# The early token tiles of the first head pair computed in float32r beside the conditioning

## The chip, the cores and the metric

The kernel runs on one core of a Trainium2 chip. TensorE (PE) multiplies matrices, VectorE (DVE), ScalarE (ACT) and GpSimd (POOL) do the elementwise work, and SyncE (SP) issues the loads and stores. The metric is the device time of one execution in microseconds (us). The kernel before takes 982.68 us, the median of three runs (982.2 to 984.94).

## The reference

One inference step of a diffusion layer: 128 prompt tokens and 1024 sample tokens, 1024 features, in float32. What matters for the front of the kernel:

```
a = silu(cond) @ w_ada + b_ada              # shift, scale, gate; one row per kind of token
h = rmsnorm(x) * norm_g * (1 + scale) + shift
q, k, v, ... = split(h @ w_in)              # 8 heads of 64 for q, k and v
q = rmsnorm(q per head) * q_norm_g ;  k = rmsnorm(k per head) * k_norm_g
```

q, k and v then go into windowed attention (sample tokens) or full attention (prompt tokens). Fourier mixing, pooling, gates and the output projection follow; the change does not touch them.

## The kernel before

The 1152 tokens are nine tiles of 128 (tiles 0 to 7 are sample tokens, tile 8 is the prompt). The front part runs once, before attention:

- *Loads* (one SP queue, in the written order): the small vectors, sixteen pieces of w_ada (`wa`, 512 KB each, for shift and scale), nine x tiles (`xt`, 512 KB), the four raw weight pieces of pair 0 (`wr_q`, 384 KB), and the first context keys and values (`kall`, `vall`).
- *Conditioning:* `ada_piece` multiplies silu(c) by a piece of w_ada in float32 (L398). After four pieces `ada_row` (ScalarE, L404) copies the row out as `ar`, `ada_end` turns it with four small matmuls `pb` (L410), and VectorE makes `sh` and `gs` (L416 to L419), shift and gain of two of the eight feature blocks k.
- *x:* `xnorms` squares a tile on ScalarE (L366) and takes the root on GpSimd (L367, L368); `xscale` scales it on VectorE (L372); `x_group` transposes three tiles at a time on TensorE (L385) into `xT`, by copies on VectorE and ScalarE (L386).
- *h:* `h_full` applies `gs` and `sh` (L451, L453). `scale_h` (L424 to L439, with the small matmuls `pbd` and `pbs`) finds from all of `gs` and `sh` one power of two, `shs`. `make_h` splits h times shs into two float16 parts: `hh` on ScalarE (L457), `hl` on VectorE (L458).
- *Weights:* `prep` squares the pieces (L86), gets a scale, and splits them into float16 parts (L112, L113).
- *Projection:* each product is three matmuls, high by high, high by low and low by high (L164 to L166). Pair 0 (two heads; q, k and v columns together 384) takes its first five token tiles at once, block k by block k, in five PSUM banks. `p1_done` then squares q and k (`sq`, L280), splits v (L281, L292), takes roots (`ss` L288, GpSimd L289 to L291), normalizes (`tk`, L295) and splits into float16 (`tok`, L302 on ScalarE, L305 on VectorE).

Tiles 8, 5, 6 and 7 of pair 0 follow one at a time. The tokens of the first four tiles are turned by transposes `pq` (L643) and `pk` (L658) as soon as their `tok` is ready, and attention starts.

The kernel is written under a manual schedule from before the loads on: every engine runs its instructions in the order of the program text. Each engine works off its queue in order, and the engines wait for each other by semaphores. `head_scales` (L479 to L494) and `v_scales` (L463 to L474) find the scales of cached keys and values with small matmuls between (`pkm`, `pks`, `pvm`, `pvs`); `new_pair` (L242 to L253) makes the constants of a pair.

Of the kernel before, what the change touches and what calls it, by code (L numbers as in the profile page):

```python
# [20 lines left out]
P = 128  # L21
# [14 lines left out]
NWA = 6  # L36
# [3 lines left out]
def mixer_layer(ctx: ExitStack, tc: tile.TileContext, xs, xp, smalls, qgrow, kgrow, bgate, wss, wgate, w1, w3, pw, wo,  # L40
# [74 lines left out]
    def prep(pieces, name):  # L115
# [3 lines left out]
        for i, src in enumerate(pieces):  # L119
            n = src.shape[-1]  # L120
            raw = wp.tile([P, WU], F32, tag="wr", name=f"wr_{name}{i}", bufs=NR)
            nc.sync.dma_start(raw[:, :n], src)
            raws.append(raw[:, :n])
        yield unit
# [56 lines left out]
    G.memset(mhalf, -0.5)  # L181

# [12 lines left out]
    with tc.tile_pool(name="hp", bufs=1, side="right") as hp:  # L195
        hh, hl = [], []
        for i in range(2):
            hh.append(hp.tile([P, 4, NT], F16, name=f"hh{i}"))
            hl.append(hp.tile([P, 4, NT], F16, name=f"hl{i}"))
# [28 lines left out]
        with tc.tile_pool(name="qkv", bufs=1) as qkv:  # L228
# [40 lines left out]
            def p1_done(c, t, pt, wait):  # L269
# [57 lines left out]
            man = ExitStack()  # L327
            man.enter_context(tc.manual_schedule())


            with tc.tile_pool(name="st", bufs=1) as st:
# [12 lines left out]
                def load_x(t):  # L344
                    xt[t] = st.tile([P, D], F32, tag="xt", name=f"xt{t}", bufs=6)
# [30 lines left out]
                XG = ((0, 1, 2), (3, 4, 5), (6, 7, 8))  # L376
                xT = st.tile([P, KT, NT], F32, name="xT")

                def x_group(ts):

                    n = len(ts) * P
                    for k in range(KT):
                        pt = bank(("s", "pt", "s")[k % 3], f"xt{k}_{ts[0]}")
                        for i, t in enumerate(ts):
                            T.transpose(pt[:, i * P:(i + 1) * P], xt[t][:, k * P:(k + 1) * P], ident)  # L385
                        (V.tensor_copy if k % 2 == 0 else S.copy)(xT[:, k, ts[0] * P:ts[0] * P + n], pt[:, :n])  # L386
# [3 lines left out]
                def ada_piece(i):  # L390
                    b, j = divmod(i, 4)
                    if j == 0:
                        pas[b] = bank("p1", f"pa{b}")
# [27 lines left out]
                def scale_h():  # L421
# [5 lines left out]
                    V.scalar_tensor_tensor(ab[:, 3:4], ab[:, 1:2], 31.0, ab[:, 2:3], op0=ALU.mult, op1=ALU.add)  # L427
                    pb = bank("po", "pbd")
# [4 lines left out]
                    V.tensor_scalar(md, ident[:2, :2], m1, None, op0=ALU.mult)  # L433
                    pb2 = bank("po", "pbs")
# [6 lines left out]
                    return hm  # L441

# [1340 lines left out]
```

## Time and profile before

| | |
|---|---|
| median of three runs | 982.68 us |
| profiled execution | 982.22 us |
| its span | 980.4 us |
| mean granted TensorE clock | 0.987 |
| TensorE busy | 918.3 us (94%) |
| VectorE busy | 656.3 us (67%) |
| ScalarE busy | 488.8 us (50%) |
| GpSimd busy | 202.4 us (21%) |

The profile is of one execution. Busy time is a share of the whole span; a stage of 100 us at the front can look quite different. Granted clock 1.00 stands for 2.4 GHz on TensorE, 0.50 for 1.2 GHz. A row of a timeline gives start, duration, engine, line, operation, output and inputs, and in brackets the idle time of the engine before it and what ended it. The duration of a matmul covers its way through a pipeline; the distance of two starts tells how fast they follow each other.

### The profile page before, as it was taken

How to read it: one execution, taken by the hardware profiler on the slowest of the kernel's cores; microseconds unless marked ns; L12 is line 12 of the kernel's file. 1: busy time of each engine (PE TensorE's matmuls, PEld its weight loads, DVE VectorE, ACT ScalarE, POOL GpSimd, SP SyncE). 2: the span in 40 equal slices, each digit the busy share in tenths (PEclk: the TensorE clock that was granted, in tenths of full speed). 3: DMA queues.
4: the chain of work that ended last, by engine and by line, in shares of the span. 5: the costliest groups of instructions: out<-in, count | busy, mean ns of one | idle time of the engine just before them, and what ended most of it. 6: DMA issues, size and time to landing. Idle time of an engine off the chain costs nothing.

```text
span 980.4 us, 17726 instructions
## 1 busy us (share of the span) xinstructions
PE 918.3 (94%) x6554; PEld 677.2 (69%) x6554; DVE 656.3 (67%) x1453; ACT 488.8 (50%) x1019; POOL 202.4 (21%) x340
## 2 busy tenths in 40 slices
PE   4778899999999999998997999999999999999998
PEld 2334467666666666665776779888888888877886
DVE  2348767777777546559778767478978789775322
ACT  2354757756856655665545545454555454442100
POOL 0000665245255322003102200002021020200000
PEclk9988999999999999999999999999999999999999
DMA  7730352151151151260249974543543432227321
GB/s 303 277 109 10 97 154 54 48 183 34 44 145 33 41 159 54 91 204 1 58 134 295 308 259 174 188 134 104 155 127 119 126 106 81 74 94 276 114 76 54
DMA packets 75783, 125.02 MB, mean 128 GB/s; under 512 B 12032, under 2 KB 45228, under 8 KB 75696
## 3 DMA queue, kind: packets, MB, share of 16 engines
q1 hardware_dynamic: 75695, 123.89, 39.2%
q8 instruction: 51, 0.84, 0.4%
q14 instruction: 37, 0.30, 0.1%
HBM read 88.20 MB, written 29.11 MB: 120 GB/s over the span
## 4 chain that ended last, share of the span: by engine, by line
PE 74%; DMA 8%; DVE 7%; ACT 5%; issue 3%; POOL 1%; SPq 1%; ACTq 0%; DVEq 0%; POOLq 0%
PE p L166 3%; PE p L164 3%; PE p L165 3%; PE wo L164 3%; PE wo L166 3%; PE wo L165 3%; PE m L164 3%; PE m L166 3%; PE m L165 3%; PE xc L164 3%; PE xb L164 3%; PE xb L166 3%; PE xb L165 3%; PE xc L165 3%; PE xc L166 3%; PE xa L164 3%
## 5 line engine op out<-in xcount | busy, mean ns | idle before, releaser
L164 PE MATMUL p<-wh_q,hh 128*128 128x384 f16 x288 | 95.1, 330 | 1.9 <-ACT hh L457 1.9
L166 PE MATMUL p<-wh_q,hl 128*128 128x384 f16 x288 | 95.0, 330 | 1.1 <-DVE hl L458 1.1
L165 PE MATMUL p<-wl_q,hh 128*128 128x384 f16 x288 | 95.1, 330 | 0.0
L733 DVE CUSTOM_DVE_ANT_0 sn<-s,bias 128x512 f32<-128x512 f32 x64 | 44.0, 688 | 31.4 <-PE s L729 30.5
L164 PE MATMUL m<-hh,wh_m 128*128 128x384 f16 x192 | 62.6, 326 | 0.0
L166 PE MATMUL m<-hh,wl_m 128*128 128x384 f16 x192 | 62.6, 326 | 0.0
L165 PE MATMUL m<-hl,wh_m 128*128 128x384 f16 x192 | 62.6, 326 | 0.0
L164 PE MATMUL wo<-woh,mh 128*128 128x512 f32 x144 | 56.8, 394 | 1.7 <-ACT woh L1536 1.7
L165 PE MATMUL wo<-wol,mh 128*128 128x512 f32 x144 | 56.6, 393 | 0.0
L166 PE MATMUL wo<-woh,ml 128*128 128x512 f32 x144 | 56.4, 392 | 0.0
L754 ACT CAST pts<-pt 128x512 f16<-128x512 f32 (+1 forms) x72 | 39.7, 552 | 29.2 <-PE pt L752 27.8
L758 DVE TENSOR_TENSOR pts<-pt,pts 128x512 f16<-128x512 f32 (+1 forms) x72 | 46.3, 642 | 3.7 <-ACT pts L754 3.1
L744 ACT ACTIVATE sn<-sn,mn 128x512 f32<-128x512 f32 x64 | 46.2, 722 | 3.9 <-DVE mn L733 3.9
L95 POOL TENSOR_SCALAR wsc_g<-wsc_g 128x1 f32<-128x1 f32 x12 | 2.6, 218 | 219.1 <-DVE wsc_g L94 219.1
L1665 DVE TENSOR_TENSOR yo<-wo,gb 128x512 f32<-128x512 f32 x18 | 12.4, 691 | 50.1 <-PE wo L166 50.0
L777 DVE TENSOR_SCALAR yt<-po,ri,vf 128x64 f32<-128x64 f32 x72 | 24.8, 344 | 29.7 <-PE po L773 26.4
L166 PEld LDWEIGHTS <-hl 128*128 128x128 f16 x288 | 28.4, 99 | 20.9 <-DVE hl L458 1.8
L164 PEld LDWEIGHTS <-hh 128*128 128x128 f16 x288 | 28.8, 100 | 19.0 <-ACT hh L457 2.0
L166 PEld LDWEIGHTS <-wl_m 128*128 128x128 f16 x288 | 28.3, 98 | 18.6 <-issue 0.4
L164 PEld LDWEIGHTS <-wh_m 128*128 128x128 f16 x288 | 28.9, 100 | 17.2 <-issue 0.6
L290 POOL TENSOR_TENSOR rs<-rs,mhalf 128x4 f32<-128x4 f32 x36 | 39.9, 1108 | 3.0
L165 PEld LDWEIGHTS <-hh 128*128 128x128 f16 x288 | 28.5, 99 | 17.1 <-issue 0.8
(650 smaller groups left out, 2942.5 us busy)
## 6 DMA issues: line engine op xcount, KB each, us to landing
wa<-in_wss_dram SPq DMA_DIRECT2D x16, 512.0 KB, 6.5
wr_q<-in_w_dram SPq DMA_DIRECT2D x16, 384.0 KB, 4.4
wr_m<-in_w_dram SPq DMA_DIRECT2D x24, 256.0 KB, 3.0
pp_c<-pec SPq DMA_DIRECT2D x24, 192.0 KB, 5.1
pp_b<-peb SPq DMA_DIRECT2D x24, 192.0 KB, 3.9
pp_a<-pea SPq DMA_DIRECT2D x24, 192.0 KB, 1.8
ppxc<-pp_c SPq DMA_DIRECT2D x16, 288.0 KB, 3.4
ppxb<-pp_b SPq DMA_DIRECT2D x16, 288.0 KB, 2.6
```

Source lines behind the costliest of these rows:

```text
L95: G.tensor_scalar(sc_[:, 2:3], sc_[:, 2:3], 1e-36, None, op0=ALU.max)
L164: T.matmul(out, lh, rh, start=first, stop=False)
L165: T.matmul(out, lh, rl, start=False, stop=False)
L166: T.matmul(out, ll, rh, start=False, stop=last)
L290: G.tensor_tensor(rs, rs, mhalf, op=ALU.pow)
L733: V.tensor_tensor_reduce(out=sn, in0=pS, in1=bt.rearrange("p a b -> p (a b)"), op0=ALU.add, op1=ALU.min, scale=1.0, scalar=3e38, accum_out=mn)
L744: S.activation(e[:, :n], it["sn"], AF.Exp, bias=it["mn"], scale=-1.0, accum_out=sm_)
L754: S.copy(pts[:, 0, :n], pt[:, :n])
L758: V.tensor_tensor(pts[:, 1, :n], it["pt"][:, :n], pts[:, 0, :n], op=ALU.subtract)
L777: V.tensor_scalar(yt[:, hd * 64:hd * 64 + 64], po[:, :64], ri, c["un"], op0=ALU.mult, op1=ALU.mult)
L1665: V.tensor_tensor(yo, pt, gb[0 if t == 8 else 1][:, cols], op=ALU.mult)
```

## The change

The first five token tiles of pair 0 (`NE` = 640 columns) no longer wait for all of the conditioning. For each block k, as soon as its `sh` and `gs` are there, `h_early` modulates 640 columns on VectorE (L468) and splits them into a float32r pair `eh` (ScalarE, L473) and `el` (VectorE, L476); `w_split` does the same with the raw weights (L491, L492). A float32r pair needs no scale. `p1_r` multiplies them in the same three matmuls, 128x384 (L168 to L170), and the steps k=0 to 7 stand between the pieces of the conditioning and the transposes.

x is transposed in groups of two, three, two and two tiles (a pair of tiles with two blocks k to a bank). There are four buffers for pieces of w_ada instead of six and five for x instead of six; `kall` and `vall` go into x buffers, and the loads are reordered. h in float16 is made after the early tiles, in the memory that `eh` and `el` leave: `make_h` on 512 columns (tiles 5 to 8), then on the early 640 (L483, L484), which pairs 1 to 3 read. The early tiles' roots are taken from unscaled products, with one more GpSimd multiply each (`gi`, L295). The manual schedule starts only behind all this; before it a scheduler orders the instructions.

```
-NWA = 6
+NWA = 4
+NE = 5 * P
...
+                    if "gi" in c:
+                        G.tensor_scalar(rs, rs, c["gi"], None, op0=ALU.mult)
...
-            man = ExitStack()
-            man.enter_context(tc.manual_schedule())
...
+                def x_group(ts, tags):
+                    n = len(ts)
+                    kk = 2 if n == 2 else 1
+                    for k in range(0, KT, kk):
+                        pt = bank(tags[nx[0] % len(tags)], f"xt{k}_{ts[0]}")
+                        for j in range(kk):
+                            for i, t in enumerate(ts):
+                                o = (j * n + i) * P
+                                T.transpose(pt[:, o:o + P], xt[t][:, (k + j) * P:(k + j + 1) * P], ident)
+                        (V.tensor_copy if nx[0] % 2 == 0 else S.copy)(xT[:, k:k + kk, ts[0] * P:(ts[0] + n) * P],
+                                                                       pt[:, :kk * n * P].rearrange("p (a b) -> p a b", a=kk))
+                        nx[0] += 1
...
+                def h_early(ks):
+                    for k in ks:
+                        h_part(k, slice(0, NE), 1)
+                        S.copy(ek(k)[0], xT[:, k, :NE])
+                    for k in ks:
+                        hi, lo = ek(k)
+                        V.tensor_tensor(lo, xT[:, k, :NE], hi.bitcast(F32), op=ALU.subtract)
+                def make_h(k, a):
+                    S.activation(hk(hh, k, a), xT[:, k, a], AF.Copy, scale=shs)
+                    V.scalar_tensor_tensor(hk(hl, k, a), xT[:, k, a], shs, hk(hh, k, a), op0=ALU.mult, op1=ALU.subtract)
...
+                def w_split(i, raw):
+                    hi = st.tile([P, WU], F32R, tag="wrh", name=f"wrh{i}", bufs=2)
+                    lo = st.tile([P, WU], F32R, tag="wrl", name=f"wrl{i}", bufs=2)
+                    S.copy(hi, raw)
+                    V.tensor_tensor(lo, raw, hi.bitcast(F32), op=ALU.subtract)
+                    wr_[i] = hi, lo
+                def p1_r(pt, t, k, first, last):
+                    eh, el = ek(k)
+                    a = slice(t * P, (t + 1) * P)
+                    b = slice((k % 2) * CH, (k % 2) * CH + CH)
+                    hi, lo = wr_[k // 2]
+                    mm3(pt[:, :CH], eh[:, a], el[:, a], hi[:, b], lo[:, b], first, last)
...
+                free = ("pt", "s", "p1")
+                ada(0, 1)
+                norm((0, 1))
+                ada(2, 3)
...
+                x_group((0, 1), free)
...
+                norm((2, 3, 4))
+                ada(4, 5, 6)
+                x_group((2, 3, 4), free)
+                w_split(0, raws[0])
+                h_early((0, 1))
+                ada(7)
...
+                pts = [bank(ebank[t], f"p1_0_{t}") for t in range(early)]
+                step(0)
...
+                w_split(1, raws[1])
+                h_early((2, 3))
+                norm((5, 6))
+                run(prep0, 4)
+                ada(8)
+                step(1)
+                ada(9)
+                step(2)
+                ada(10, 11)
...
+                x_group((5, 6), ("po",))
+                step(3)
...
+                w_split(2, raws[2])
+                h_early((4, 5))
...
+                norm((7, 8))
+                ada(12, 13)
+                step(4)
+                ada(14, 15)
...
+                wu0 = wu = run(prep0, 4)
+                x_group((7, 8), ("po",))
+                head_scales(kall)
+                v_scales(vall)
+                step(5)
...
+                w_split(3, raws[3])
+                h_early((6, 7))
...
+                    h_late(k, (S, V)[k % 2])
+                sc = scale_h()
+                next(sc)
...
+                        p1_r(pts[t], t, k, False, k == KT - 1)
+                    if t == 1:
+                        next(sc)
+                    if t == 3:
+                        next(sc, None)
+                ectx.close()
+                hp = hctx.enter_context(tc.tile_pool(name="hp", bufs=1, side="right", reuse_waits="tile"))
+                for i in range(2):
+                    hh.append(hp.tile([P, 4, NT], F16, name=f"hh{i}"))
+                    hl.append(hp.tile([P, 4, NT], F16, name=f"hl{i}"))
+                h_late(6, S)
+                h_late(7, V)
+                inverse_of(wu["sc"])
+                c0 = new_pair(0, wu)
+                gi = pers.tile([P, 1], F32, name="gi")
+                V.reciprocal(gi, wu["inv"])
+                c0e = dict(c0, gi=gi, i8=eighth, sv=c0["scv"])
+                for k in range(KT):
+                    make_h(k, slice(NE, NT))
+                for t in range(early):
+                    tick()
+                    tick()
+                    p1_done(c0e, t, pts[t], 8)
+                for k in range(KT):
+                    make_h(k, slice(0, NE))
+            man = ExitStack()
+            man.enter_context(tc.manual_schedule())
```

What the scheduler makes of it on TensorE, in the stretch of pieces 9 to 15 of the conditioning. In `pa2`, `pa3` the pieces' rows grow, `pb` turns them, `p1_0_0` is the bank of pair 0's tile 0. Before:

```order
L398 MATMUL pa2_337<-wa9_158,sil_83 32x512 x2
L398 MATMUL pa2_337<-wa10_160,sil_83 32x512 x2
L398 MATMUL pa2_337<-wa11_162,sil_83 32x512 x2
L410 MATMUL pb2_399<-pick_84,ar2_397 128x2 x4
L398 MATMUL pa3_421<-wa12_172,sil_83 32x512 x2
L130 MATMUL pw_q0_424<-wss_q0_408,onesp_75 128x4
L398 MATMUL pa3_421<-wa13_174,sil_83 32x512 x2
L398 MATMUL pa3_421<-wa14_176,sil_83 32x512 x2
L398 MATMUL pa3_421<-wa15_178,sil_83 32x512 x2
L410 MATMUL pb3_447<-pick_84,ar3_445 128x2 x4
```

After (numbers of buffers left out; `p_0_4` is tile 4's bank, `xt_5` a transposed bank of tiles 5 and 6):

```order
L168 MATMUL p_0_4_314<-wrh_339,eh_344 128x384
L405 MATMUL pa_371<-wa_158,sil 32x512 x2
L169 MATMUL p_0_4_314<-wrl_340,eh_344 128x384
L170 MATMUL p_0_4_314<-wrh_339,el_345 128x384
L390 MATMUL xt_5_412<-ident,xt_152 128x128
L390 MATMUL xt_5_412<-ident,xt_154 128x128
L390 MATMUL xt_5_412<-ident,xt_152 128x128
L390 MATMUL xt_5_412<-ident,xt_154 128x128
L168 MATMUL p_0_0_310<-wrh_339,eh_348 128x384
L169 MATMUL p_0_0_310<-wrl_340,eh_348 128x384
L170 MATMUL p_0_0_310<-wrh_339,el_349 128x384
```

Pieces that followed each other now stand alone between float32r matmuls of steps 2 and 3 and the transposes of tiles 5 and 6; before, no projection stood ahead of the last piece.

On VectorE, from the last `hl` to the first roots of pair 0's tiles, before (`gs4`, `grow` and `vf` are the pair's constants, `ss` the sums for the roots):

```order
L458 SCALAR_TENSOR_TENSOR hl1_98<-xT_121,shs_77,hh1_97 128x1152 x3
L242 TENSOR_SCALAR gs40_631<-qs__89,wsc_q0_428 128x2
L243 TENSOR_TENSOR grow0_630<-qgb_87,gs40_631 128x128
L242 TENSOR_SCALAR gs40_631<-ks__90,wsc_q0_428 128x2
L243 TENSOR_TENSOR grow0_630<-kgb_88,gs40_631 128x128
L247 TENSOR_SCALAR vf0_636<-wsc_q0_428 128x1
L248 TENSOR_TENSOR vf0_636<-vrec_79,wsc_q0_428 128x1
L249 TENSOR_TENSOR vf0_636<-vf0_636,svb_78 128x1
L90 TENSOR_SCALAR vf0_636<-vf0_636 128x1
L251 RECIPROCAL vf0_636<-vf0_636 128x1
L252 TENSOR_TENSOR vf0_636<-vf0_636,wsc_q0_428 128x1
L253 RECIPROCAL vf0_636<-vf0_636 128x1
```

After, where the 640-wide `hl` stand:

```order
L484 SCALAR_TENSOR_TENSOR hl1_692<-xT_114,shs_77,hh1_691 128x512
L256 RECIPROCAL vf0_705<-vf0_705 128x1
L484 SCALAR_TENSOR_TENSOR hl1_692<-xT_114,shs_77,hh1_691 128x512 x3
L297 SCALAR_TENSOR_TENSOR v160_713<-p1_0_0_310,vf0_705,v160_713 128x2x64
L297 SCALAR_TENSOR_TENSOR v160_713<-p1_0_1_311,vf0_705,v160_713 128x2x64
L297 SCALAR_TENSOR_TENSOR v160_713<-p1_0_2_312,vf0_705,v160_713 128x2x64
L297 SCALAR_TENSOR_TENSOR v160_713<-p1_0_3_313,vf0_705,v160_713 128x2x64
L300 TENSOR_TENSOR tk0_0_736<-p1_0_0_310,rg0_0_735 128x256
L484 SCALAR_TENSOR_TENSOR hl0_690<-xT_114,shs_77,hh0_689 128x640 x4
L484 SCALAR_TENSOR_TENSOR hl1_692<-xT_114,shs_77,hh1_691 128x640 x4
L291 TENSOR_REDUCE ss0_4_790<-sq0_4_789 128x4
```

All eight 640-wide `hl` now stand between the first `tk` and the first `tok` of the early tiles, and the 512-wide ones ahead of the early tiles' v; before, the last `hl` stood ahead of the pair's constants.

## Rows read from the trace of the kernel before

**Rows 1.** The page: engines' busy time, and a row of its DMA issues.

```profile
PE 918.3 (94%) x6554; PEld 677.2 (69%) x6554; DVE 656.3 (67%) x1453; ACT 488.8 (50%) x1019; POOL 202.4 (21%) x340
...
mk<-in_masks_dram SPq DMA_DIRECT2D x1, 576.0 KB, 3.3
```

**Rows 2.** Busy time by stretches: start:end, length, engines, granted clock, DMA share, GB/s.

```profile
48.00:64.00 16.00, 12.41 (x48) 6.01 (x48) 7.70 (x18) 8.89 (x17) 0.00 (x0) 0.92 0.36 99
75.00:78.00 3.00, 1.87 (x6) 0.68 (x7) 2.96 (x5) 3.00 (x3) 0.00 (x0) 0.50 0.00 0
96.15:115.25 19.10, 17.05 (x107) 10.09 (x105) 13.63 (x49) 12.05 (x31) 13.38 (x22) 1.00 0.50 133
```

**Rows 3.** Waits from 96 to 123: us in total, times, the longest.

```profile
PE pq L643 <- DVE tok L305: 1.6, 1, 1.6
...
PE pk L658 <- ACT q L645: 1.1, 1, 1.1
```

**Rows 4.** Timeline, VectorE and pq from 92 to 116: start, us, engine, line.

```profile
92.17 4.07 DVE L458 SCALAR_TENSOR_TENSOR hl<-xT,shs,hh 128x1152 f16<-128x1152 f32 x3
...
98.11 0.16 DVE L253 RECIPROCAL vf<-vf 128x1 f32<-128x1 f32 x1
...
104.34 0.42 DVE L305 TENSOR_TENSOR tok<-tk,tok 128x256 f16<-128x256 f32 x1 [0.47 <-ACT tok L302]
106.42 0.42 DVE L288 TENSOR_REDUCE ss<-sq 128x4 f32<-128x256 f32 x1 [1.66 <-ACT sq L280]
...
114.82 0.40 DVE L305 TENSOR_TENSOR tok<-tk,tok 128x256 f16<-128x256 f32 x1
115.28 0.45 PE L643 MATMUL pq<-id,tok 128*128 128x128 f16 x5 [1.64 <-DVE tok L305]
```

**Rows 5.** Timeline, ScalarE from 73 to 109.

```profile
73.71 3.55 ACT L457 ACTIVATE hh<-xT,shs 128x1152 f16<-128x1152 f32 x3 [3.01 <-DVE shs L90]
...
101.95 0.48 ACT L280 ACTIVATE sq<-p,vf 128x256 f32<-128x256 f32 x1 [0.24 <-PE p L166]
...
108.53 0.38 ACT L611 ACTIVATE kh<-kr,ks__90 128x128 f16<-128x128 f32 x1
```

**Rows 6.** Timeline of the conditioning and x, from 10 to 69.

```profile
10.72 1.06 ACT L366 ACTIVATE xsq<-xt 128x1024 bf16<-128x1024 f32 x1 [7.42 <-DMA xt<-in_xs_dram]
...
14.58 3.20 PE L398 MATMUL pa<-wa,sil 128*32 128x512 f32 x8 [3.20 <-DMA wa<-in_wss_dram]
...
15.83 2.08 DVE L372 TENSOR_SCALAR xt<-xt,xss 128x1024 f32<-128x1024 f32 x3 [11.76 <-POOL xss L368]
...
44.24 1.92 PE L398 MATMUL pa<-wa,sil 128*32 128x512 f32 x4
...
54.87 1.54 PE L385 MATMUL xt<-ident,xt 128*128 128x128 f32 x6 [0.57 <-ACT xT L386]
...
56.34 2.71 PE L398 MATMUL pa<-wa,sil 128*32 128x512 f32 x12
...
60.49 1.05 PE L410 MATMUL pb<-pick,ar 128*128 128x2 f32 x8 [1.43 <-ACT ar L404]
...
64.81 3.60 PE L398 MATMUL pa<-wa,sil 128*32 128x512 f32 x12
```

**Rows 7.** Timeline, TensorE at 147: float32 transposes of 128x128 (attention).

```profile
147.67 0.60 PE L752 MATMUL pt<-ident,sn 128*128 128x128 f32 x4
148.11 0.25 PE L773 MATMUL po<-v,pts 128*128 128x64 f16 x3
```

**Rows 8.** Timeline, TensorE at 447: float32r matmuls of 128x384 (the pooling branch).

```profile
446.99 0.34 PE L165 MATMUL yc<-dl,wph 128*128 128x384 f32 x1
447.16 0.34 PE L166 MATMUL yc<-dh,wpl 128*128 128x384 f32 x1
```

**Rows 9.** Timeline, VectorE: start and end of the head and value scales.

```profile
82.35 1.19 DVE L479 TENSOR_REDUCE km<-kall 64x8 f32<-64x1024 f32 x1
...
92.09 0.16 DVE L474 COPY vrec<-pvs 128x4 f32<-128x4 f32 x1 [0.47 <-PE pvs L473]
```

More of the change, by code (lines that the diff above doesn't have):

```diff
@@ L113, in split16, with prep @@
         V.scalar_tensor_tensor(lo, raw, sc_[:, 0:1], hi, op0=ALU.mult, op1=ALU.subtract)
-    def prep(pieces, name):
+    def prep(pieces, name, halves=False):
         unit = {"w": []}
@@ L123, in prep @@
             raws.append(raw[:, :n])
+            if halves and i == 1:
+                yield unit
+        unit["raws"] = raws
         yield unit
@@ L181, in mixer_layer @@
     G.memset(mhalf, -0.5)
+    eighth = pers.tile([P, 1], F32, name="eighth")
+    G.memset(eighth, 0.125)
     col = pers.tile([P, 44], F32, name="col")
@@ L193, in mixer_layer @@
     kb_ = pers.tile([P, 8], F32, name="kb_")
-    with tc.tile_pool(name="hp", bufs=1, side="right") as hp:
+    with ExitStack() as hctx:
         hh, hl = [], []
-        for i in range(2):
-            hh.append(hp.tile([P, 4, NT], F16, name=f"hh{i}"))
-            hl.append(hp.tile([P, 4, NT], F16, name=f"hl{i}"))
         def hk(z, k, a):
@@ L375, in mixer_layer @@
                 ebank = ["p1", "p1", "p1", "s", "pt"]
-                XG = ((0, 1, 2), (3, 4, 5), (6, 7, 8))
                 xT = st.tile([P, KT, NT], F32, name="xT")
[L379 to L386, printed above, removed]
+                nx = [0]
+                def x_group(ts, tags):
[10 more added lines that the diff above has]
+                        nx[0] += 1
                 pas = {}
@@ L455, in make_h, with ek @@
-                def make_h(k):
-                    a = slice(0, NT)
-                    S.activation(hk(hh, k, a), xT[:, k], AF.Copy, scale=shs)
-                    V.scalar_tensor_tensor(hk(hl, k, a), xT[:, k], shs, hk(hh, k, a), op0=ALU.mult, op1=ALU.subtract)
+                ectx = ExitStack()
+                ep = ectx.enter_context(tc.tile_pool(name="ep", bufs=1, side="right", reuse_waits="tile"))
+                ets = {}
+                def ek(k):
+                    if k not in ets:
+                        ets[k] = [ep.tile([P, NE], F32R, tag=x, name=f"{x}{k}", bufs=6) for x in ("eh", "el")]
+                    return ets[k]
@@ L494, in head_scales @@
                     V.tensor_copy(kb_, pks[:, :8])
-                prep0 = prep_pair(0)
-                wu0 = None
-                for what in ("w0", "w1", 0, 1, 2, "w2", "w3", 3, 4, 5, "w4", "w5", "w6", "w7", 6, 7, 8, "w8", "w9", "w10", "w11"):
-                    load_x(what) if isinstance(what, int) else load_wa(int(what[1:]))
-                run(prep0, 1)
-                for i in range(12, 16):
-                    load_wa(i)
-                kall = st.tile([64, 4, 2, P], F32, tag="wa", name="kall", bufs=NWA)
+                prep0 = prep([w1[0, i] for i in range(4)], "q0", True)
@@ new lines, in mixer_layer @@
+                for what in ("w0", "w1", 0, 1, "w2", "w3", 2, 3, 4, "r", "w4", "w5", "w6", "w7", "r", 5, 6, "w8", "w9", "w10", "w11",
+                             7, 8, "w12", "w13", "w14", "w15"):
+                    if isinstance(what, int):
+                        load_x(what)
+                    elif what == "r":
+                        r0 = run(prep0, 1)
+                    else:
+                        load_wa(int(what[1:]))
+                raws = r0["raws"]
+                kall = st.tile([P, D], F32, tag="xt", name="kall", bufs=5)[:64].rearrange("p (a h t) -> p a h t", a=4, h=2)
@@ new lines, in mixer_layer @@
+                h_late(6, S)
[7 more added lines that the diff above has]
+                    make_h(k, slice(NE, NT))
+                for t in range(early):
+                    tick()
+                    tick()
+                    p1_done(c0e, t, pts[t], 8)
```

91 lines of the change are left out of this document (22 added, 69 removed).

## The prediction, made before the result was known

> **What bounds the kernel now.** I read the page first: TensorE is busy for 918.3 of the 980.4 us of the span [rows 1], and after the first eighth that hardly varies. Whatever a change at the front wins must be found at the front. The busy time by stretches came next [rows 2]: TensorE works 12.41 of the 16 us from 48 to 64, at a rate looked at below. In the stretch 96.15 to 115.25 it has 17.05 of 19.1, VectorE 13.63 of the same 19.1. Third, TensorE's waits from 96 to 123 [rows 3]: the longest is 1.6 us, the transposes pq of pair 0's tokens waiting for VectorE's tok; the next is 1.1. Fourth, the timeline there [rows 4]: the fourth tok (tile 3) is issued at 114.82 and done at 115.22, and pq goes on at 115.28. From pq on both kernels run the same instructions in the same order (hl and hh are complete by then in both), so the change in time is, to first order, the change in when that tok ends. The reader should see that VectorE's queue, not the last matmul of the early tiles at about 101.9 [rows 5], opens that gate.
>
> **The change part by part.** All prices come from the profiled execution, 982.22 us (span 980.4); the median shown is 982.68, so 0.46 is added at the end.
>
> 1. *Until the transposes of tiles 2 to 4.* Two x tiles are loaded ahead of pieces 2 and 3 instead of three. Those pieces, waiting for their load, ended at 17.8 (14.58 + 3.20 [rows 6]); one tile less, about 1.3 of loading, gives 16.4. 16 transposes at 0.26 (six in 1.54 [rows 6]) end at 20.7. ScalarE squares tiles 2 to 4 from 19.8; three squares and GpSimd's two steps took from 10.72 to 15.83 [rows 6], and one copy (0.6) now stands between: 25.5. The first scaling (0.7, a third of 2.08 [rows 6]) gives 26.2.
>
> 2. *The interleaved stretch, steps k=0 to 5.* TensorE gets 56 transposes, 90 float32r matmuls, ten lone pieces and a pair, and two pb groups. At the upper clock: transposes 0.11 each (147.67 to 148.11 for four [rows 7]), 6.2; float32r passes of 128x384 0.17 to 0.175 (446.99 to 447.16 [rows 8]), 15.8; pb 2 x 1.05 = 2.1. A lone piece took 1.92 [rows 6] at the slow rate, three together 3.60; I halve the first as an estimate for ten lone ones and a pair, 11 x 0.96 = 10.6. Sum 34.7. What the clock does is the choice here. The profile prints 1.00 until 58, yet the same transposes go at 0.26 there and at 0.11 later [rows 6, 7], and 12 ada matmuls take 2.71 at 56.34 and 3.60 at 64.81 [rows 6]. So I read the first 56 us as the lower level (1.2 GHz), and the engine rose near 57 after a stretch of dense transposes from 48 on (12.41 busy of 16). The new stretch is at least as dense from 26.2. It could rise at once or after 10 us; I take 4.5, which do 2.25 us of work. 26.2 + 4.5 + 32.4 + 2.4 for two waits (ar, pb and VectorE's sh/gs behind a piece; 1.43 is one wait for ar [rows 6]) = 65.5. Were everything slow, it would be 26.2 + 69 + 2.4 = 98.
>
> The Trainium skill ("TensorE: Matmul & The Clock Gate", Part 4: PE-mode transpose) says that transposes do not engage the faster clock, as they do not count as busy "the same way". Here the rise near 57 came right behind transposes (the last six at 54.87 [rows 6]), so the trace speaks against it; by the page the interleaved stretch would stay slow longer, as in rival C.
>
> 3. *The scale chain.* After the last transposes VectorE runs copies, the head and value scales (82.35 to 92.25 in before, with TensorE round trips [rows 9]) and the modulation of the late columns between; a pb group stands behind the value scale in TensorE's order. I take 9.5, and k=6 begins at 75.
>
> 4. *k=6 and 7.* 30 float32r matmuls, begun after waits and so at the lower level: about 20 at 0.35 (twice 0.175, as 0.50 was granted from 75 to 78 behind a wait [rows 2]) and ten at 0.175, with pbd and pbs 0.84: 9.4. The early tiles end at 84.4, 17 us before they did; shs is there at 84.1.
>
> 5. *What is late next: VectorE.* The f16 pairs hh, hl were made under the early matmuls (hl 8 x 1.36, three in 4.07 [rows 4]); that cover is gone, because they now need shs, which comes when the early matmuls are over. They stand in the order between the early tiles' roots and toks, as the order excerpts show. A hl of 512 costs 0.69 and one of 640 0.83 (1.36 for 1152 [rows 4], less a fixed 0.16 or so, by width). From 84.1: twelve small instructions at 0.2 (eleven lie between the hl's end at 96.24 and 98.27 [rows 4]) to 86.5; eight hl of 512 and five small ones, 6.5, to 93.0; four v (0.30) and a tk, 1.6, to 94.6; eight hl of 640, 6.6, to 101.2. Then ss and v of tile 4, tok 0, tk and tok 1 with ScalarE's cast between: 103.0, against 104.76 before [rows 4]. From there to tok 3 the instructions are the same; they took 10.46, in which VectorE waits 1.66 for tile 8's squares [rows 4]. Those squares now wait on ScalarE behind a cast and a weight square, not for TensorE, and come about 0.4 sooner. tok 3 ends at 113.0, and pq starts 2.2 us earlier.
>
> 6. *Hidden.* Tile 8 is paced by the 512-wide hl, about 7 us in place of 3.9, but TensorE then waits for tok in any case. GpSimd gets a multiply per early tile (0.25) while its results are needed 8 us later. The two additional casts of ScalarE per k (8 x 0.55 + 8 x 0.68 for hh, from 1.18 per 1152, three in 3.55 [rows 5]) stay under VectorE's 13. Weights: fewer buffers, but pieces 8 to 15 have 8 us and more between the release of a buffer and the matmul that wants it. If that cover is gone, a late landing shows as some 3 us in step 2 or 3.
>
> 7. *TensorE's clock at the gate.* It idles for some 10 us before pq, so the matmuls behind pq may begin at the lower level. In 75 to 78, behind a wait, 0.50 was granted [rows 2]. The price is 0 to 2 us, and half of it lies under the wait of 1.1 that follows pq [rows 3]; I take 0, by the row of 96 to 115 (1.00 in spite of a wait), and leave 2 in the range.
>
> 8. *Loads behind the last hl.* Masks and cached keys are issued when the last hl is done (96.24 before, about 101 now). The masks took 3.3 us to land, and ScalarE used the keys behind them at 108.53 [rows 1, 5]; now it would want them near 106, 5 us after the issue. If they land in that time it costs nothing; when they landed before no row shows, so it could be late by up to 7. I take 0.5, near the masks' row.
>
> Sum: 982.22 - 2.2 + 0.5 = 980.5 on the profiled execution, 981.0 against the median.
>
> **The rivals.** A is the forecast: VectorE's 13 us of late hl take back almost all of TensorE's 17. For it: 13.63 of 19.1 was already busy. Its own range is 978.5 to 983.5 (2.5 us of waits either way).
>
> B, a larger gain: the clock is up at 26 and steps 3 and 4 are shorter (k=6 and 7 warm, 5.3 + 0.84 for 9.4), so early tiles end near 80; VectorE's queue starts 4.5 earlier and with it pq: 982.7 - 1.7 - 4.5 = 976.5. For it: five tiles' worth of dense matmuls; against it: the lower level whenever TensorE waited (75 to 78 [rows 2]).
>
> C, slower: TensorE stays at 1.2 GHz in the interleaved stretch until about 45 in place of 30.7. Then 14.3 more us do half the work, +7.1: early end 91.5, pq 7.1 - 1.7 = 5.4 later than before, 988.1. It decides from an early end later than 86.1, where VectorE's tail reaches 115.22 again. Slow all through, k=6 would begin near 107 and the time be 1012. For it: the lower level from 0 to 56 in before; against it: the rise at 57.
>
> D, that the early work gains nothing: the waits of steps 2 to 4 (scales, pb behind pvs, a late piece) cost 3 us more than taken, or the toks queue that much behind ScalarE's hh; VectorE's tail ends at 116 to 117 and the time is 984. For it: an order fixed ahead with many small round trips. Against: most of these waits lie beside 34.7 us of other work.
>
> **How the numbers follow.** A 0.36, B 0.26, C 0.18, D 0.20. 0.3%, 2.95 us, is what a measurement can tell. Under A faster than 979.7 in a third of its cases, else within; B faster; C slower in all but 0.02; D within in 0.14 of 0.20, slower in the rest. Faster 0.12 + 0.26 = 0.38, same 0.24 + 0.02 + 0.14 = 0.40, slower 0.16 + 0.06 = 0.22. The likeliest is A, 981.0, with its own range 978.5 to 983.5. For 8 in 10 the range goes from 971.5 (B with another 5 us) to 989 (C).
>
> **What would show it.** Transposes of tiles 2 to 4 starting near 26; their spacing falling from 0.26 to 0.11 near 31; step 5 ending near 65 and k=6 beginning near 75; squares of tile 4 near 84; VectorE with 13 us of hl at L484 between 86 and 101, without gaps; TensorE's wait for tok before pq of over 4 us instead of 1.6; pq resumed near 113.5. The forecast is wrong if pq waits for something else, if the early tiles end outside 80 to 88, or if the spacing of pq to the end of the span differs from before.

## The result

The changed kernel takes 976.55 us, the median of six runs (974.96 to 978.04), against 982.44 (980.59 to 986.56) for the kernel before: a ratio of 0.9928, 95% interval 0.9902 to 0.9953, so 6 to 7 us faster. A second set of runs (after_again below) gave 0.9962 (0.9948 to 0.9976), about 4 us. The time lies inside the predicted range and the gain is larger than the likeliest case had it: 981.0 was forecast there. That the first set meets rival B's 976.5 almost exactly is partly chance, as the second set shows.

The profiled execution has a span of 973.2 us against 980.4. The page's busy times, which answer to [rows 1]:

```profile
PE 910.5 (94%) x6554; PEld 679.9 (70%) x6554; DVE 665.1 (68%) x1478; ACT 496.9 (51%) x1039; POOL 208.2 (21%) x348
```

TensorE has about the share it had; VectorE works 8.8 us more than before; its new work of `el` (6.3 us in all) and `wrl` (3.8) is about that much. Busy time by stretches, in the columns of [rows 2]:

```profile
26.00:40.00 14.00, 14.00 (x80) 9.77 (x79) 9.49 (x19) 8.57 (x18) 0.00 (x0) 0.88 0.83 305
40.00:66.00 26.00, 24.64 (x134) 15.29 (x132) 16.58 (x28) 14.71 (x25) 3.60 (x6) 1.00 0.57 165
66.00:75.00 9.00, 3.42 (x16) 3.13 (x17) 6.91 (x32) 3.26 (x6) 0.00 (x0) 0.74 0.00 0
75.00:85.00 10.00, 8.60 (x41) 6.57 (x41) 6.62 (x29) 5.95 (x11) 5.93 (x10) 0.89 0.00 0
95.00:105.00 10.00, 2.38 (x9) 1.36 (x10) 7.18 (x20) 5.58 (x16) 4.20 (x7) 0.50 0.62 161
```

From 26 to 66 TensorE is nearly full (38.64 of 40 us) and at the upper level after its first few us. From 66 to 75 it works 3.42 of 9: the scale chain. From 95 to 105 it works 2.38 of 10 and 0.50 is granted: it stands at `pw_q` (below) while VectorE makes the late hl. TensorE's timeline at the places the prediction named:

```profile
25.38 2.01 PE L390 MATMUL xt<-ident,xt 128*128 128x128 f32 x8 [4.84 <-DVE xt L374]
27.32 1.94 PE L405 MATMUL pa<-wa,sil 128*32 128x512 f32 x8
29.19 1.52 PE L390 MATMUL xt<-ident,xt 128*128 128x128 f32 x11
30.64 1.05 PE L405 MATMUL pa<-wa,sil 128*32 128x512 f32 x4
...
34.12 0.34 PE L169 MATMUL p<-wrl,eh 128*128 128x384 f32 x1
34.29 0.34 PE L170 MATMUL p<-wrh,el 128*128 128x384 f32 x1
...
64.94 0.34 PE L170 MATMUL p<-wrh,el 128*128 128x384 f32 x1
...
69.92 1.45 PE L417 MATMUL pb<-pick,ar 128*128 128x2 f32 x8
73.90 0.69 PE L168 MATMUL p<-wrh,eh 128*128 128x384 f32 x1 [2.53 <-ACT eh L473]
74.39 0.53 PE L169 MATMUL p<-wrl,eh 128*128 128x384 f32 x1
74.71 0.53 PE L168 MATMUL p<-wrh,eh 128*128 128x384 f32 x1
...
81.19 0.34 PE L170 MATMUL p<-wrh,el 128*128 128x384 f32 x1
...
102.62 0.59 PE L134 MATMUL pw_q<-wss_q,onesp 128*128 128x4 f32 x2 [10.50 <-ACT wjk_q L87]
...
109.84 0.61 PE L711 MATMUL pq<-id,tok 128*128 128x128 f16 x8
...
115.96 0.40 PE L742 MATMUL pqp<-id,tok 128*128 128x128 f16 x4 [0.68 <-DVE tok L310]
...
134.00 0.38 PE L797 MATMUL s<-ka,q 128*128 128x512 f16 x1
```

Transposes of tiles 2 to 4 begin at 25.38; eight take 2.01 there and eleven take 1.52 at 29.19, so the rise to the upper level lies early among those eleven, behind the two pieces at 27.32. Step 5's last matmul is issued at 64.94, k=6 begins at 73.90, the early tiles' last matmul is issued at 81.19, 20 us ahead of before [rows 5]. Then VectorE's queue, the counterpart of [rows 4]:

```profile
80.70 0.15 DVE L91 TENSOR_SCALAR shs<-shs 128x1 int32<-128x1 int32 x1
...
82.51 0.73 DVE L484 SCALAR_TENSOR_TENSOR hl<-xT,shs,hh 128x512 f16<-128x512 f32 x1
...
90.58 6.80 DVE L484 SCALAR_TENSOR_TENSOR hl<-xT,shs,hh 128x640 f16<-128x640 f32 x8
97.30 0.41 DVE L291 TENSOR_REDUCE ss<-sq 128x4 f32<-128x256 f32 x1
...
99.10 0.42 DVE L310 TENSOR_TENSOR tok<-tk,tok 128x256 f16<-128x256 f32 x1 [0.47 <-ACT tok L307]
100.30 0.42 DVE L291 TENSOR_REDUCE ss<-sq 128x4 f32<-128x256 f32 x1 [0.77 <-ACT sq L283]
...
107.92 0.41 DVE L310 TENSOR_TENSOR tok<-tk,tok 128x256 f16<-128x256 f32 x1
```

The tok of tile 3 ends at 108.33 where it ended at 115.22, 6.9 us earlier. Of TensorE's 20 us two thirds are gone by then. pq did not wait for it: TensorE came to pq only at 109.84, because pw_q had waited 10.50 us for the squares of pair 1's weights. Those stand on ScalarE behind the casts of the toks, which wait for VectorE. Waits from 82 to 140 (columns of [rows 3]):

```profile
PE pw_q L134 <- ACT wjk_q L87: 10.5, 1, 10.5
...
PE pqp L742 <- DVE tok L310: 0.7, 1, 0.7
```

The counterparts of the last two rows before:

```profile
122.68 0.40 PE L674 MATMUL pqp<-id,tok 128*128 128x128 f16 x4 [0.87 <-DVE tok L305]
...
140.71 0.38 PE L729 MATMUL s<-ka,q 128*128 128x512 f16 x1
```

The wait of pk is gone and that of pqp, the transposes of the prompt tile's q, has stayed, so the lead is again VectorE's at pqp: it comes at 115.96 against 122.68, and the first attention scores (the first matmul that writes `s` from `ka` and `q`) at 134.00 against 140.71, both 6.7 us earlier.

### The profile page after: what moved, and what is told of

It reads as the page before. It is cut to its first block, busy times and chain, and to the rows that moved or that the text cites. A ratio compares the mean times of both kernels' runs of the same rounds, so it can differ in the third digit from the quotient of the medians.

```text
span 973.2 us, 17777 instructions
## 1 busy us (share of the span) xinstructions
PE 910.5 (94%) x6554; PEld 679.9 (70%) x6554; DVE 665.1 (68%) x1478; ACT 496.9 (51%) x1039; POOL 208.2 (21%) x348
## 4 chain that ended last, share of the span: by engine, by line
PE 76%; DVE 9%; DMA 6%; ACT 4%; issue 2%; SPq 2%; POOL 1%; DVEq 0%; POOLq 0%; ACTq 0%
PE p L168 4%; PE p L169 4%; PE p L170 4%; PE wo L168 3%; PE wo L170 3%; PE wo L169 3%; PE xc L168 3%; PE xb L168 3%; PE xb L169 3%; PE xc L169 3%; PE xc L170 3%; PE xb L170 3%; PE m L168 3%; PE m L170 3%; PE m L169 3%; PE xa L168 3%
## 5 line engine op out<-in xcount | busy, mean ns | idle before, releaser
L170 PE MATMUL p<-wh_q,hl 128*128 128x384 f16 x248 | 81.9, 330 | 2.5 <-DVE hl L484 2.3
L168 PE MATMUL p<-wh_q,hh 128*128 128x384 f16 x248 | 81.9, 330 | 0.2 <-ACT hh L483 0.2
L169 PE MATMUL p<-wl_q,hh 128*128 128x384 f16 x248 | 81.8, 330 | 0.0
L168 PE MATMUL m<-hh,wh_m 128*128 128x384 f16 x192 | 62.6, 326 | 0.0
L170 PE MATMUL m<-hh,wl_m 128*128 128x384 f16 x192 | 62.6, 326 | 0.0
L168 PE MATMUL wo<-woh,mh 128*128 128x512 f32 x144 | 56.9, 395 | 1.8 <-ACT woh L1604 1.8
L170 PE MATMUL wo<-woh,ml 128*128 128x512 f32 x144 | 56.5, 392 | 0.0
L822 ACT CAST pts<-pt 128x512 f16<-128x512 f32 (+1 forms) x72 | 39.8, 552 | 29.6 <-PE pt L820 28.2
L170 PEld LDWEIGHTS <-wl_m 128*128 128x128 f16 x288 | 28.2, 98 | 18.4 <-issue 0.2
L168 PEld LDWEIGHTS <-wh_m 128*128 128x128 f16 x288 | 28.8, 100 | 17.0 <-issue 0.4
L169 PEld LDWEIGHTS <-wh_m 128*128 128x128 f16 x288 | 28.2, 98 | 16.9 <-issue 0.5
L170 PEld LDWEIGHTS <-hl 128*128 128x128 f16 x248 | 24.5, 99 | 21.7 <-DVE hl L484 5.1
L820 PE MATMUL pt<-ident,sn 128*128 128x128 f32 x256 | 38.5, 273 | 0.0
```

The costliest lines, as they stand in the source:

```text
L168: T.matmul(out, lh, rh, start=first, stop=False)
L169: T.matmul(out, lh, rl, start=False, stop=False)
L170: T.matmul(out, ll, rh, start=False, stop=last)
L820: T.transpose(pt[:, j * P:(j + 1) * P], it["e"][:, j * P:(j + 1) * P], ident)
L822: S.copy(pts[:, 0, :n], pt[:, :n])
```

## The experiments

All ratios are to the kernel before on the same chip. Single executions of one kernel spread by 1 to 10 us, so the place of an effect is read from the profile and its size at the end from the ratio. The slower executions of a kernel are mostly those with the lower mean granted clock: in pb_first, 0.982 to 0.984 goes with 971.59 to 973.74 us and 0.975 to 0.979 with 975.02 to 979.56. The milestones, in us, from the profiled execution of each ("last matmul" is the start of it; tile 3 is taken to be the fourth tok in VectorE's order):

| kernel | early tiles' last matmul | last hl ends | tok of tile 3 ends | first scores | time ratio (95%) |
|---|---|---|---|---|---|
| before | about 101.5 | 96.24 | 115.22 | 140.71 | 1 |
| changed | 81.19 | 97.38 | 108.33 | 134.00 | 0.9928 (0.9902 to 0.9953) |
| after_again | 81.92 | 98.11 | 109.07 | 134.81 | 0.9962 (0.9948 to 0.9976) |
| twice_hl640 | 81.47 | 104.03 | 114.98 | 140.90 | 1.0021 (1.0002 to 1.0041) |
| no_hl640 | 81.88 | 90.09 (zeros until 93.84) | 104.84 | 130.32 | 0.9932 (0.9906 to 0.9958) |
| pb_first | 75.16 | 92.99 | 103.65 | 129.42 | 0.9934 (0.9911 to 0.9957) |
| wjk_first | 84.78 | 100.99 | 111.39 | 136.98 | 0.9975 (0.9952 to 0.9999) |
| toks_first | 81.47 | 101.87 | 94.64 | 135.70 | 0.9967 (0.9955 to 0.9979) |
| both_first | 75.00 | 99.15 | 94.84 | 133.25 | 0.9960 (0.9940 to 0.9980) |
| keys_early | 74.96 | 99.10 | 94.79 | 129.07 | 0.9895 (0.9865 to 0.9925) |
| text_order | 91.40 | 110.02 | 121.60 | 147.09 | 1.0100 (1.0080 to 1.0121) |
| text_pb_first | 80.82 | 105.38 | 116.97 | 142.45 | 1.0052 (1.0032 to 1.0072) |
| before_sched | 91.41 | 80.65 | 106.00 | 131.48 | 0.9935 (0.9914 to 0.9957) |
| before_bufs | 97.02 | 91.68 | 110.67 | 136.15 | 0.9978 (0.9957 to 0.9998) |

**after_again.** 

> The changed kernel once more, unaltered, beside the next three on the same chip, since single executions of one kernel spread by 8 us here. Expected 0.99 to 0.995 of the kernel before, with the early tiles ending near 81, tok of tile 3 near 108.3 and the first attention scores near 134.0, as in its first profile. If these milestones move by more than 1 us, differences of the front read from one profile are worth less than taken.

The milestones moved by 0.7 to 0.8 us, and the ratio, 0.9962, is a little above the 0.99 to 0.995 that were expected. In the five profiles whose edits lie behind the early tiles or that have none, the early end lies between 81.19 and 81.92, so differences of the front above 1 us can mostly be read; a different level of TensorE's clock can move a front further (wjk_first and before_bufs below).

**twice_hl640**: `make_h` on the early columns is followed by

```
+                    V.scalar_tensor_tensor(hk(hl, k, slice(0, NE)), xT[:, k, :NE], shs, hk(hh, k, slice(0, NE)), op0=ALU.mult, op1=ALU.subtract)
```

> The changed kernel with each of the eight 640-wide hl computed twice on VectorE, so 8 x 0.83 = 6.7 us more in its queue between the first tk and the first tok. Theory 1 (VectorE's queue from shs to the toks decides, so the late hl take back what TensorE gained): tok of tile 1 ends near 106.2 instead of 99.5, the prompt's transposes pqp go about 6.5 us later, time +6 to +7 against the changed kernel, about 983, level with the kernel before. Theory 2 (VectorE has slack there, and TensorE's cold tile 5 behind its 10.5 us wait for the weight squares decides): at most +3.

```profile
94.41 1.67 DVE L484 SCALAR_TENSOR_TENSOR hl<-xT,shs,hh 128x640 f16<-128x640 f32 x2
96.00 1.67 DVE L642 SCALAR_TENSOR_TENSOR hl<-xT,shs,hh 128x640 f16<-128x640 f32 x2
...
105.76 0.42 DVE L310 TENSOR_TENSOR tok<-tk,tok 128x256 f16<-128x256 f32 x1 [0.47 <-ACT tok L307]
```

VectorE's timeline: tok of tile 1 ends at 106.18 instead of 99.52, and 6.7 us more in that queue are 6.9 us at the first scores. Theory 1 holds; the time is 1.0021 (1.0002 to 1.0041), level with the kernel before.

**no_hl640**: the low half of h is left out for the first five tiles, and zeros are written in its place.

```
-                    make_h(k, slice(0, NE))
+                    S.activation(hk(hh, k, slice(0, NE)), xT[:, k, :NE], AF.Copy, scale=shs)
+                    V.memset(hk(hl, k, slice(0, NE)), 0.0)
```

> The changed kernel with the eight 640-wide hl left out (the low half of h of the first five tiles is set to zero, which later pairs read). Theory 1: VectorE reaches the first tok about 5 us earlier, but ScalarE's eight 640-wide hh end only at 94.2, so tok of tile 1 ends near 95.8 instead of 99.5 and all behind moves by that: time -3 to -4 against the changed kernel, about 973. Theory 2 (TensorE decides): tile 5 waits for the weight squares, which also come earlier, so -2 to -4 as well; what tells them apart is the run with hl twice. If VectorE's late work costs nothing, 0.

In the front it went as theory 1 had it: first scores 3.7 us earlier. The ratio does not show it (0.9932, where about 0.989 would follow). In this profile 844.8 us lie between the first scores and the end, in the changed kernel's 839.2; ScalarE's longest wait for a later pair's cached keys was 2.7 instead of 1.1 us, and TensorE's for the gate weights 5.7 in all instead of 2.4. Whether loads that come closer together cause these waits or chance does, stays open.

**pb_first**: the last block of the conditioning ahead of step 5, the scales of cached keys and values behind the early tiles.

```
-                head_scales(kall)
-                v_scales(vall)
-                step(5)
                 ada_end(3)
                 w_split(3, raws[3])
                 h_early((6, 7))
+                step(5)
...
+                head_scales(kall)
+                v_scales(vall)
                 ectx.close()
```

> The changed kernel with the last block of the conditioning (pb of pieces 12 to 15, sh and gs, eh and el of k=6, 7) written ahead of step 5, and the scales of cached keys and values behind the early tiles. In the changed kernel TensorE ran from 65.3 to 73.9 almost empty, with pb behind the value scale. Theory 1 (that order in the scale chain costs TensorE 8 us, and the early end sets VectorE's queue): k=6 begins near 66, warm, the early tiles end near 72 to 73, shs near 72; the moved scales (about 3 us of VectorE) go into its tail, so toks about 5 us earlier, time -4 to -5.5, about 971.5. Rival (VectorE's tail takes it back: the scales' two round trips now stall it, and its queue was free for only some 5 us between 64 and 82): early end as early, but time 0 to -2.

The early tiles end 6 us earlier and the first scores come 4.6 us earlier, as theory 1 had it for the front; k=6 began at 67.84, not 66. The time shows none of it (0.9934), as in no_hl640: 846.3 us lie between first scores and end.

**wjk_first**: in pair 0's steps the four squares of pair 1's weights are issued first.

```
-                            when = [2 * n for n in range(2, 13)]
+                            when = [0, 0, 0, 0] + [2 * n for n in range(6, 13)]
```

> The changed kernel with the four squares of pair 1's weights taken out from between the toks' casts on ScalarE; they fall into ScalarE's gap near 67 to 71. Theory 1 (they hold TensorE for 10.5 us before pw_q, tile 5 then runs at 0.50 and pq comes 1.5 us behind its tok; and they hold tile 8's squares and the cached keys on ScalarE): tile 5 runs right behind tile 8 until about 96 at the upper level, pq goes with tok of tile 3 near 106 to 107, time -1.5 to -3, about 974. Rival (the cached keys' load, issued behind the last hl at 97.8, lands only near 102 and holds ScalarE then): 0 to -1.

```profile
95.57 0.28 PE L134 MATMUL pw_q<-wss_q,onesp 128*128 128x4 f32 x2
109.28 0.48 PE L711 MATMUL pq<-id,tok 128*128 128x128 f16 x3 [9.02 <-DVE wsc_q L95]
111.44 0.71 PE L711 MATMUL pq<-id,tok 128*128 128x128 f16 x5 [1.69 <-DVE tok L310]
```

TensorE's wait for the squares is gone, and the same time is waited at pq, for VectorE's reduction of pw_q (9.02), which stands in its queue behind the cached keys, and for tok. From the early end to the first scores it took 52.2 instead of 52.8. The theory fell: TensorE's idle time there cost almost nothing, VectorE's order set it. (This execution, 984.43 us, was the slowest of its kernel's twelve, which begin at 975.94. The early tiles themselves ended 3.6 us later, 2.0 of it before the moved squares: the granted clock from 54 to 60 was 0.72 where the changed kernel had 1.00, and ScalarE's copy of the last ar began at 62.97 instead of 60.93.)

**toks_first**: all steps of the early tiles are issued before the 640-wide `make_h`.

```
                     p1_done(c0e, t, pts[t], 8)
+                while steps["todo"]:
+                    tick()
                 for k in range(KT):
                     make_h(k, slice(0, NE))
```

> The changed kernel with the early tiles' tk and tok written ahead of the 640-wide hh and hl; the same instructions, so VectorE has as much to do. Theory 1a (it is the order, toks behind eight hl, that holds the transposes): tok of tile 3 ends near 96 instead of 108.3, pq follows tile 5 (near 103 or earlier), pqp goes near 110 instead of 115.96, first scores 3 to 6 us earlier; time -3 to -5. Theory 1b (it is VectorE's amount of work, in whatever order, which the prompt tile's tok, the cached keys behind the last hl and the first scores wait for): tok of tile 3 as early, but the first scores at 133 to 134 and time 0 to -1.

```profile
99.61 0.19 ACT L87 ACTIVATION_READ_ACCUMULATOR wjk_q<-wr_q 128x1 f32 x1
106.32 0.69 ACT L681 ACTIVATE kh<-kr,ks__92 128x128 f16<-128x128 f32 x2 [6.52 <-DMA kr<-in_kctx_dram]
```

The fourth tok came 13.7 us earlier and nothing was won: the first scores came at 135.70 and the time is 0.9967 against after_again's 0.9962 on the same chip. That is theory 1b in its outcome, by another cause than the amount of work. ScalarE now waits 6.52 us for the cached keys, whose load is issued at 102.28, behind the last hl (101.87). This is the term that step 8 of the prediction had bounded; in the changed kernel the load landed in time (kh at 102.48, right behind the squares).

**both_first**: pb_first and toks_first together.

> pb_first and toks_first together. In pb_first the first scores came at 129.4, 4.6 us before the changed kernel's 134.0, and the gain was not seen in the time. If the two add in the front: first scores at 125 to 127. If what is won in the front reaches the end: time 7 to 9 under the changed kernel on the same chip, about 968. If attention gives it back (waits for the loads of each pair's cached keys, which were up to 1.7 us longer in pb_first), half of that or less.

First scores at 133.25, not 125 to 127: the two do not add, since ScalarE's wait for the same load grew to 8.9 us.

**keys_early**: both_first, and the cached keys of pair 0 loaded with the first loads.

```
+                kr0 = qkv.tile([P, 2, P], F32, tag="kr", name="kr0", bufs=1)
+                nc.sync.dma_start(kr0, kctx[0])
...
-                            at_(14, cached_v, c)
+                            at_(18, cached_v, c)
```

> both_first with pair 0's cached keys loaded with the first loads, into memory that h does not use (before, kr was issued behind the last hl and ScalarE waited 8.9 us for it), and cached_v four steps later. Theory (with the toks early, the load behind the last hl is the next wait; it holds ScalarE, the cached keys on VectorE, and pq through pair 1's weight scale): kh near 95 instead of 103.87, VectorE's kl right behind the last hl near 100 instead of 104.3, first scores 3.5 to 5 us earlier, near 129. Rival (VectorE's 7 us of late hl bind by themselves): first scores 0 to 1.5 us earlier. If the front's gain reaches the end, time 4 under both_first, about 0.992 of the kernel before.

```profile
94.84 0.68 ACT L685 ACTIVATE kh<-kr,ks__92 128x128 f16<-128x128 f32 x2
...
98.52 0.47 ACT L283 ACTIVATE sq<-p,vf 128x256 f32<-128x256 f32 x1 [2.99 <-PE p L170]
```

kh no longer waits, the first scores come 4.2 us before both_first's, and this kernel has the lowest time of the study: 972.58 us, 0.9895 (0.9865 to 0.9925), clear of both_first and after_again and not of the changed kernel's first 0.9928. The edit also puts the cached values four steps later, which was not tried by itself.

**text_order**: the manual schedule again from before the loads on, in the changed kernel.

```
+            man = ExitStack()
+            man.enter_context(tc.manual_schedule())
             with tc.tile_pool(name="st", bufs=1) as st:
...
-            man = ExitStack()
-            man.enter_context(tc.manual_schedule())
```

> The changed kernel with the manual schedule from the start, as in the kernel before: every engine in the order of the text. Theory 1 (the gain comes from projecting the early tiles beside the conditioning, whoever orders it): early tiles end within 4 us of 81.2, time within 3 us of the changed kernel. Rival (the gain comes from the scheduler's order): text order blocks at each round trip (scales of cached keys, pb, pbd and pbs with nothing between), the early tiles end at 90 or later and the time is at or above the kernel before.

```profile
56.00:66.00 10.00, 6.87 (x31) 4.79 (x31) 6.01 (x10) 7.07 (x11) 1.76 (x4) 0.83 0.07 18
66.00:75.00 9.00, 4.46 (x16) 3.10 (x17) 6.07 (x20) 1.42 (x3) 0.00 (x0) 0.53 0.21 70
75.00:82.00 7.00, 5.88 (x22) 5.79 (x21) 1.01 (x5) 0.00 (x0) 0.00 (x0) 0.50 0.00 0
82.00:92.00 10.00, 7.86 (x34) 6.61 (x35) 7.26 (x24) 6.10 (x12) 0.00 (x0) 0.75 0.00 0
```

The rival holds for this text. From 66 to 82 TensorE is half empty or at 0.50; the early tiles end at 91.4 and the time is 1.0% above the kernel before. The text was written for the scheduler; whether a hand-written order made for the early tiles would do better was not tried, except for one chain:

**text_pb_first**: pb_first under the manual schedule.

> pb_first in the order of the text from the start, no scheduler. In text_order TensorE waited with the last pb for the scales of cached keys and values and ran at 0.50 from 66 to 82. Theory 1 (that one chain is what text order loses): early tiles end near 78 to 80 instead of 91.4, first scores near 134 to 136 instead of 147.1, time within 0.3% of the changed kernel. Rival (text order blocks in many places): early end at 85 or later, first scores at 140 or later, time at or above the kernel before.

Mending that one chain gave the early tiles' end 10.6 us and the first scores 4.6 us, and left the time above the kernel before, as the rival had it. The early tiles now end as in the changed kernel (80.82), and shs is issued as early (80.35). What is lost stands behind them: VectorE first makes the moved scales of cached keys and values and the pair's constants, so the first hl of 512 starts at 89.94 instead of 82.51.

**before_sched**: the kernel before, its manual schedule begun only behind the early tiles, as in the change.

```
-            man = ExitStack()
-            man.enter_context(tc.manual_schedule())
             with tc.tile_pool(name="st", bufs=1) as st:
...
+            man = ExitStack()
+            man.enter_context(tc.manual_schedule())
             yT_d = dr.tile([4, P, NT], F32, name="yT_d")
```

> The kernel before with nothing changed but that the order up to attention is left to the scheduler. Theory 1 (the scheduler's order only pays with the new text, which gives TensorE the early tiles' matmuls to put between): early tiles end within 3 us of 101.8, time within 0.3% of the kernel before. Rival (the scheduler alone makes most of the gain): early tiles end 5 us or more earlier, time -4 to -7.

```profile
64.00:75.00 11.00, 7.58 (x28) 4.05 (x29) 9.65 (x28) 7.86 (x9) 0.00 (x0) 0.54 0.00 0
75.00:95.50 20.50, 20.50 (x128) 12.26 (x127) 11.50 (x32) 6.86 (x16) 5.17 (x9) 1.00 0.50 121
```

The rival holds here too: 0.9935 (0.9914 to 0.9957), as much as the whole change, and the first scores come 2.5 us before the changed kernel's. shs is issued at 67.84 instead of 73.52, three of the four small matmuls of the scales go before the early tiles instead of among them, the last hl ends at 80.65 instead of 96.24, and from 75 to 95.5 TensorE works 20.50 of 20.5 us, where the kernel before worked 17.41. Not all of that is the order: in before_bufs, in the order of the text, shs is issued at 68.73 as well. Against that profile the scheduler's order still has the last hl 11.0 us, the end of the early tiles 5.6 and the first scores 4.7 us earlier.

**before_bufs**: the kernel before with `NWA = 4` and five x buffers.

> The kernel before with four buffers for the pieces of w_ada instead of six and five for x instead of six, its order of loads unaltered: the edit that was costed at nothing. Theory (the loads arrive early enough): the early tiles' end within 0.5 us of 101.8, time within 0.3% of the kernel before. Rival (the loads of pieces 4 to 15 now wait for buffers): early end up to 3 us later, time +1 to +3.

```profile
14.84 3.20 PE L398 MATMUL pa<-wa,sil 128*32 128x512 f32 x8 [3.21 <-DMA wa<-in_wss_dram]
17.97 2.11 PE L385 MATMUL xt<-ident,xt 128*128 128x128 f32 x9
20.73 0.88 PE L385 MATMUL xt<-ident,xt 128*128 128x128 f32 x6 [0.65 <-DVE xT L386]
21.84 0.55 PE L385 MATMUL xt<-ident,xt 128*128 128x128 f32 x3 [0.24 <-ACT xT L386]
```

Neither: TensorE waits longer for pieces (16.1 us in all, 8.7 before), and yet the first scores come 4.6 us earlier, since in this execution transposes ran at the upper level from about 20.7 and again in later stretches, where the profile of before shows the lower one until 57. The execution, 977.31 us, is one of the fast ones of its kernel (975.41 to 983.96); the time is 0.9978 (0.9957 to 0.9998), hardly different. So fewer buffers cost nothing that shows; and 4 to 5 us of the 7.2 between the two profiles may lie in the level at which TensorE passed its first 57 us in the one profile of before. The ratios, not the profiles, carry the size of the gain.

## Why the prediction was right and where it was not

**What bounds.** Right: the lead that TensorE won was settled by VectorE's queue. The tok of tile 3 came 6.9 us earlier, the first scores 6.7, the end 4 to 7. What failed is the sentence that pq would go with that tok: TensorE came 1.5 us later, held by pw_q's 10.50 us at ScalarE's squares, and the lead was settled at pqp instead. By the prediction's own list this was a sign of being wrong; it cost nothing, since ScalarE's squares and the toks wait for the same queue of VectorE.

**Steps 1 to 3** (26.2, 65.5, 75): 25.4, 65.1 and 73.9. The clock rose near 29, earlier than the 30.7 that was taken; a lone piece took 1.05 where 0.96 was estimated, a float32r pass 0.175. That the rise fell so near was in part luck, for the reason given does not hold. The prediction held that the rise near 57 came behind dense transposes, and that this speaks against the rule it cites on them. In that trace the transposes from 48.01 to 56.3 kept the lower level to their end (six in 1.54 at 54.87 [rows 6]), and the rise came inside the three pieces that follow (2.71, where twelve such matmuls took 3.60 at the lower level and, in before_bufs, 1.91 at the upper). In the changed kernel, too, two pieces stood just ahead of the rise.

**Step 4** was mis-sized: 9.4 was forecast for k=6 and 7 (its own terms add up to 9.6) and 7.3 came, since the rise came near 77.3, after some eleven matmuls and not twenty.

**Step 5** was right in its mechanism and 1.4 us too long (27.5 from shs to tok 3, not 28.9). The eight hl of 640 took 6.72 (forecast 6.6), those of 512 with the small ones 6.7 (6.5). The part from tok 1 to tok 3 took 8.8, not 10.0. twice_hl640 shows that this queue decides: 6.7 us added there come out as 6.9.

**Step 6** held for the buffers and the weights. **Step 7**: the clock did fall (0.50 from 95 to 105), and wjk_first shows that this cost next to nothing in this kernel: there tile 5 ran at the upper level, and the first scores came as long after the early end. **Step 8** was 0.5 us too high: the keys landed in time; toks_first shows that the term was real and next in line.

Together: shs 3.2 us earlier than forecast, the queue 1.4 shorter, the load's 0.5 not paid: 5.1 us, the difference between the forecast 1.7 and the 6.7 to 6.9 of the front. That is rival B's outcome, with the clock at k=6 and 7 as its cause in part. How much of the 6.7 belongs to the one profile of before, whose first 57 us were at the lower level, is open (before_bufs), so the close sum is not a proof of each term.

**What the prediction did not see** is which half of the change pays. It weighed the early float32r tiles and took the scheduler as given. The four kernels give: text order and f16 tiles 1, text order and float32r tiles 1.010, scheduler and f16 tiles 0.9935, scheduler and float32r tiles 0.9928 and 0.9962. The early tiles, with the loads, groups and buffers that belong to them, cost 1% in the text's order and under the scheduler add nothing that can be measured; leaving the order to the scheduler makes the gain. The prediction's own numbers hinted at it: TensorE's 17 us were given back almost whole by hl that had lost their cover. Whether the early tiles pay once that queue is mended, as in keys_early, is not shown, since the same mends were not tried on before_sched.

**Rival C** (TensorE slow in the interleaved stretch) did not come. Its point of decision, an early end later than about 86, is not enough to go by: text_order passed it with 91.4 and is slower than before, but text_pb_first stayed below it with 80.82 and is slower too. **Rival D's** time, 984, did not come either; that the early work gains nothing is what the four kernels show.

**Open.** Why 844.6 to 846.3 us lie between first scores and end in no_hl640, pb_first, wjk_first, text_order and text_pb_first, and 838.4 to 841.7 in the other nine profiles. Behind the first scores TensorE was granted 0.50 for 10.2 us in all in pb_first, wjk_first and text_order, and for 0 to 6.8 us in the others. At half speed 10.2 us are 5.1 us of work at most, an estimate, so the clock may have a part in these three; in no_hl640, with 3.4 us, it hardly has.

## What to carry to other kernels

When a change does work earlier and also gives up a hand-written order, run the two halves apart before crediting either. A lead on one engine is worth only what the next engine's queue lets through: list what lay under the old work, price it, and put it in that queue. And when a queue is cleared, look at the loads that are issued behind its last instruction; they are the next wait.

## What the runs showed of the hardware

- The upper level can come in the middle of transposes: in before_bufs two float32 pieces (14.84 to 18.0) are followed by nine transposes in 2.11 us from 17.97, and from 20.73 six took 0.88. In the profile of before, nine at 20.82 took 2.37 after nearly the same work. The level can thus differ between executions with nearly the same TensorE work; what decides it was not settled.
- Transposes alone brought no rise here. In the profile of before two stretches of nothing else, 31.45 to 39.8 and 48.01 to 56.3, ended as slow as they began (six in 1.54 at 38.30 and at 54.87).
- A float32r pass of 128x384 is issued every 0.176 us at the upper level and 0.32 at the lower (74.39, 74.71), a f16 pass every 0.163 and 0.32: nearly the same.
- Executions of one kernel spread by 5.5 to 10 us in sets of 10 to 32, more than most of the front's effects.
